# DMA transposes of 16-bit words in place of TensorE transposes for eight of eleven FFN blocks, in a two-layer decoder trunk

## The chip, the cores and the metric

The kernel runs on one core of a Trainium2 chip. Five engines work beside each other, each through its own queue in order: TensorE (PE, matmuls; its weight loads are shown as PEld), VectorE (DVE), ScalarE (ACT), GpSimd (POOL) and SyncE (SP, which only issues DMAs). Sixteen DMA engines move data. The metric is the device time of one execution in microseconds, of which the median of three runs is taken.

## The reference

Two layers over 256 tokens of width 2048, all in float32:

```python
for l in range(DEPTH):                                   # DEPTH = 2
    h = rms_norm(x, norm1_g[l])
    z = h @ w_in[l]                                      # 2048 -> 3584
    z_sgu = jax.nn.gelu(z[..., :2 * SGU_WIDTH], approximate=False)
    out_a = chunked_sgu(z_sgu, sgu_norm_g[l], sgu_w[l], sgu_b[l])
    out_b = swa_sink_attention(..., sinks[l], rel_bias)  # 16 heads, window 128, T5 bias
    mixed = jnp.concatenate([rms_norm(out_a, out_norm_a[l]),
                             rms_norm(out_b, out_norm_b[l])], axis=-1)
    x = x + mixed @ w_out[l]
    h2 = rms_norm(x, norm2_g[l])
    x = x + (jax.nn.silu(h2 @ w_gate[l]) * (h2 @ w_up[l])) @ w_down[l]   # width 5632
return x
```

The relative bias of a head depends on query minus key alone, so a head's 128 x 256 table is one line of values, read at a shift for each query.

## The kernel before

Every product of float32 is made of three matmuls in a reduced format (`mm3`, L143 to L146): both operands are split into a high and a low part, and high x high, high x low and low x high are added up in PSUM. Activations are split when they are made. Weights are split as they come: `raw_load` (L89) brings 512 KB (128 partitions x 1024 columns), `split2` (L96) has ACT write `wh` (a cast, L102) and DVE write `wl` (the difference, L103). There are seven `raw` buffers and five each of `wh` and `wl`. A **unit** is one such load, its split and its matmuls.

The FFN has 11 blocks of 512 hidden columns. Blocks 2 to 10 (`S_BLOCKS`) are made by `seven`, which forms both token halves with seven products of half the size in place of eight: its units (`s_unit`) have six matmuls, on tiles `m0` to `m4`, and some of its weights are sums of loads that DVE adds up (L676, L677, L685) and that a DMA from POOL adds into (L688). Blocks 0 and 1 are made by `half`, on tiles `dacc`, with standard units of 12 matmuls, and so is the down projection, `down`, over groups of one to three blocks.

When a block's gated activations `sg` (two tiles of 128 tokens x 512 columns) are ready, they must be turned, so that the hidden columns lie on the partitions, and split. `act_T` (L613) does that for half a block: four TensorE transposes into the PSUM tile `ps_f`, a cast on ACT (L617) and a subtraction on DVE (L618) that make one pair `aT`. `act_later` (L640) asks for it two and three ticks after the block. A tick is a standard unit; an `s_unit` counts half.

What runs when is decided as the program is written out. The loop at L807 takes pieces of `seven` in turn, and `debt` counts DVE's estimated time (`vec`) up and PE's (`pe`) down; while it is above zero, standard units of `std_stream` are put between, since they have much PE time for one split. A piece of `down` is possible only when both `aT` pairs of all its blocks exist (L791), and otherwise a later piece or none is taken. `held`, `room` and `admit` keep no more than six `aT` pairs alive. What was written out is then ordered on each engine by a scheduler, and each engine runs its list in order.

Once at the start, `rel_table` (L261) makes the bias: three small loads, a matmul that picks table rows (`ps_r`), an addition, a store of one line per head to DRAM (`rline`) and a skewed copy DRAM to DRAM of 2 MB (`rdram`), which `load_bias` reads with 512 KB loads, twice four in all.

At the end `down` adds `acc` to the residual `xres` and stores 256 KB pieces (L768, L771).

Of the kernel before, what the change touches and what calls it, by code (L numbers as in the profile page):

```python
# [12 lines left out]
F32 = mybir.dt.float32  # L13
F32R = mybir.dt.float32r
BF16 = mybir.dt.bfloat16
AF = mybir.ActivationFunctionType
ALU = mybir.AluOpType
AX = mybir.AxisListType
PSUM = bass.MemoryType.PSUM
DRAM = bass.MemoryType.DRAM  # L20
# [15 lines left out]
NB = 512  # L36
KT = D // P
EPS = 1e-6
NEG = -1e30
NI = 3584 // NB  # L40
NFF = DFF // NB
ND = D // NB
# [28 lines left out]
def trunk(ctx, tc, x, xt, w_in, w_out, w_gate, w_up, w_down, sgu_w, sgu_g, consts,  # L71
          rel_bias, onehot, radd, out):
    nc = tc.nc

    cp = ctx.enter_context(tc.tile_pool(name="cp", bufs=1))
# [4 lines left out]
    sp = ctx.enter_context(tc.tile_pool(name="sp", bufs=4))  # L80
    dp = ctx.enter_context(tc.tile_pool(name="dp", bufs=1, space=DRAM))
    pa = ctx.enter_context(tc.tile_pool(name="pa", bufs=5, space=PSUM))
# [3 lines left out]
    def f(t):  # L86
        return t.bitcast(F32)
# [27 lines left out]
    def pe(n):  # L115
        debt[0] -= n * MM * LOAD
# [4 lines left out]
    def later(delay, fn):  # L121
        pending.append((clock[0] + delay, next(serial), fn))
# [122 lines left out]
    xres = cp.tile([P, NTOK, D], F32, tag="xres", name="xres")  # L245
    rdram = dp.tile([NH, P, SEQ], F32, tag="rdram", name="rdram")
    pairs1 = []
# [12 lines left out]

    def rel_table():  # L261
        relb = cp.tile([NBUCKET, NH], F32, tag="relb", name="relb")
        nc.gpsimd.dma_start(relb, rel_bias)
        oneh = zp.tile([NBUCKET, RL], F32, tag="z", name="oneh")
        nc.gpsimd.dma_start(oneh, onehot)
        rad = zp.tile([NH, RL], F32, tag="z", name="rad")
        nc.gpsimd.dma_start(rad, radd)
        ps_r = small_ps([NH, RL], "ps_r")
        nc.tensor.matmul(ps_r, relb, oneh, start=True, stop=True)
        rsb = zp.tile([NH, RL], F32, tag="z", name="rsb")  # L270
        nc.vector.tensor_tensor(rsb, ps_r, rad, ALU.add)
        rline = dp.tile([NH, RL], F32, tag="rline", name="rline")
        nc.sync.dma_start(rline, rsb)
        skew = bass.AP(
            tensor=rline.tensor, offset=rline.offset + P - 1, ap=[[RL, NH], [-1, P], [1, SEQ]]
        )
        nc.sync.dma_start(rdram, skew)

    first_pair(0)
    for p in range(1, KT // 2):  # L280
        later(p, lambda p=p: first_pair(p))
    for i in range(2 * NTOK):
        later(5 + 2 * i, lambda i=i: load_x(i // 2, i % 2))
    later(11, rel_table)

    for lay in range(L):
# [75 lines left out]
        def attend(g, t, kT=kT, qT=qT, vhl=vhl, ov=ov, bias=bias, layer=layer, pts=pts):  # L362
            nkb = t + 1
            nk = nkb * P
            k0 = SEQ - nk
            G = g // 2
# [246 lines left out]
        def act_T(b, c, sg, pairs_f=pairs_f):  # L613
            ps = pm.tile([P, 2, SEQ], F32, tag="sm", name="ps_f")
            transpose_pair([sg[t][:, 2 * c * P : (2 * c + 2) * P] for t in range(NTOK)], ps)
            pair = pair_tile("aT")
            nc.scalar.copy(pair[:, 0], ps)  # L617
# [137 lines left out]
        def down(blocks, n, final, lay=lay, pairs_f=pairs_f, norm_block=norm_block, ss1=ss1,  # L755
# [10 lines left out]
            for t in range(NTOK):  # L766
                xs = xres[:, t, n * NB : (n + 1) * NB]
                nc.vector.tensor_tensor(xs, acc[t], xs, ALU.add)  # L768
                vec(1, VEC_P)
                if final and lay == L - 1:  # L770
                    nc.sync.dma_start(out[t * P : (t + 1) * P, n * NB : (n + 1) * NB], xs)  # L771
            if final and lay < L - 1:
# [135 lines left out]
```

## Time and profile before

| | |
|---|---|
| median of 3 runs | 1932.12 us (1931.79 to 1932.31) |
| the profiled execution | 1932.53 us, span 1930.8 us, granted clock 0.999 |
| busy, share of the span | PE 100%, PEld 81%, DVE 88%, ACT 60%, POOL 6% |
| DMA | 424.39 MB, 220 GB/s over the span |
| transposes of `ps_f` | 176 of 8734 matmuls |
| FFN of layer 0, of layer 1 | about 290 to 965 us, 1250 to 1926 us |

The page names an instruction by line, engine, operation and tiles (out<-in). A group shows its count, the time it was busy, the mean of one in ns and the engine's idle time just before it with what ended most of it. PE's matmuls overlap, so that one shows 0.39 us where the next starts 0.23 us later.

### The profile page before, as it was taken

The page shows a single profiled execution, that of the slowest core. Times are in us where ns is not written, and L with a number is a line of the kernel's source. Part 1 is how long each engine was busy: PE and PEld are TensorE (multiplying, and loading weights), DVE is VectorE, ACT ScalarE, POOL GpSimd, SP SyncE. Part 2 cuts the span into 40 slices and gives each one's busy share as a digit, 9 for nine tenths or more (in the row PEclk, how much of TensorE's full clock was granted, in tenths as well). Part 3 has the DMA queues.
Part 4 walks back from the last instruction along what each step waited for, and adds up shares of the span by engine and source line. Part 5 has one row for each costly group of instructions (what it writes and reads, how often), then busy time and mean ns, then how long its engine had stood idle before and what let it go on. Part 6 is the DMA issues. An engine that isn't in the chain of part 4 may idle for free.

```text
span 1930.8 us, 24275 instructions
## 1 busy us (share of the span) xinstructions
PE 1922.1 (100%) x8734; PEld 1568.0 (81%) x8734; DVE 1698.7 (88%) x1896; ACT 1162.8 (60%) x1475; POOL 122.8 (6%) x127
## 2 busy tenths in 40 slices
PE   9999999999999999999999999999999999999999
PEld 7777888888888888888888788888888888888887
DVE  6787689999999999999767866899999999999995
ACT  7476566666665665656555765666665565665662
POOL 1211000000000000000012100000000000000000
PEclk9999999999999999999999999999999999999999
DMA  8845557768768777767555445577678678768773
GB/s 324 287 156 174 175 172 253 218 218 262 220 217 260 227 225 246 227 224 248 206 205 190 162 165 186 184 240 224 214 238 241 217 240 251 231 219 246 238 240 121
DMA packets 119704, 424.39 MB, mean 220 GB/s; under 512 B 13168, under 2 KB 15344, under 8 KB 119584
## 3 DMA queue, kind: packets, MB, share of 16 engines
q1 hardware_dynamic: 106928, 377.57, 54.6%
q0 software_dynamic: 12512, 45.19, 12.7%
q8 instruction: 68, 1.11, 0.2%
q14 instruction: 52, 0.43, 0.1%
q10 hardware_dynamic: 144, 0.08, 0.0%
HBM read 420.66 MB, written 4.23 MB: 220 GB/s over the span
## 4 chain that ended last, share of the span: by engine, by line
PE 94%; DVE 3%; ACT 1%; issue 1%; DMA 1%; POOL 0%; SPq 0%; ACTq 0%; DVEq 0%; POOLq 0%
PE m L145 11%; PE m L146 11%; PE m L144 11%; PE dacc L144 10%; PE dacc L145 10%; PE dacc L146 10%; PE acc L144 9%; PE acc L146 9%; PE acc L145 9%; DVE wl L103 1%; PE ps_f L217 1%; PE ps_n L217 1%; PE ps_s L379 0%; PE ps_p L414 0%; PE ov L422 0%
## 5 line engine op out<-in xcount | busy, mean ns | idle before, releaser
L102 ACT CAST wh<-raw 128x1024 fp32r<-128x1024 f32 (+1 forms) x778 | 799.8, 1049 | 592.1 <-DVE raw L676 198.6
L103 DVE TENSOR_TENSOR wl<-raw,wh 128x1024 fp32r<-128x1024 f32 (+1 forms) x778 | 926.2, 1219 | 130.3 <-ACT wh L102 124.3
L145 PE MATMUL dacc<-wl,aT 128*128 128x512 f32 x576 | 225.4, 391 | 0.0
L144 PE MATMUL dacc<-wh,aT 128*128 128x512 f32 x576 | 224.8, 391 | 0.0
L145 PE MATMUL m<-wl,ext 128*128 128x512 f32 x576 | 224.8, 390 | 0.0
L146 PE MATMUL dacc<-wh,aT 128*128 128x512 f32 x576 | 224.6, 390 | 0.0
L144 PE MATMUL m<-wh,ext 128*128 128x512 f32 x576 | 224.5, 392 | 0.0
L146 PE MATMUL m<-wh,ext 128*128 128x512 f32 x576 | 224.3, 389 | 0.0
L103 DVE TENSOR_TENSOR wl<-t,wh 128x1024 fp32r<-128x1024 f32 x144 | 175.6, 1222 | 25.1 <-ACT wh L102 21.5
L102 ACT CAST wh<-t 128x1024 fp32r<-128x1024 f32 x144 | 151.2, 1052 | 57.8 <-PE dacc L146 37.9
L144 PE MATMUL acc<-wh,hT 128*128 128x512 f32 x448 | 179.5, 402 | 0.4 <-ACT pt L415 0.4
L145 PE MATMUL acc<-wl,hT 128*128 128x512 f32 x448 | 175.2, 391 | 1.1 <-DVE wl L103 1.1
L146 PE MATMUL acc<-wh,hT 128*128 128x512 f32 x448 | 175.2, 391 | 0.0
L144 PE MATMUL m<-wh,hT 128*128 128x512 f32 x432 | 168.5, 390 | 0.1
L145 PE MATMUL m<-wl,hT 128*128 128x512 f32 x432 | 168.1, 389 | 0.0
L146 PE MATMUL m<-wh,hT 128*128 128x512 f32 x432 | 168.1, 389 | 0.0
L144 PE MATMUL acc<-wh,aT 128*128 128x512 f32 x384 | 152.0, 396 | 0.0
L146 PE MATMUL acc<-wh,aT 128*128 128x512 f32 x384 | 150.0, 391 | 0.0
L145 PE MATMUL acc<-wl,aT 128*128 128x512 f32 x384 | 149.7, 390 | 0.0
L688 POOL DMA_DIRECT2D t<-in_w_gate_dram x72 | 61.3, 852 | 1326.1 <-DVE wl L103 828.3
L145 PEld LDWEIGHTS dacc<-wl,aT 128*128 128x128 f32 x576 | 108.2, 188 | 24.1 <-DVE wl L103 2.2
L144 PEld LDWEIGHTS dacc<-wh,aT 128*128 128x128 f32 x576 | 108.1, 188 | 23.8 <-DVE xres L768 1.4
(150 smaller groups left out, 2809.0 us busy)
## 6 DMA issues: line engine op xcount, KB each, us to landing
raw<-in_w_gate_dram SPq DMA_DIRECT2D x176, 512.0 KB, 5.5
raw<-in_w_up_dram SPq DMA_DIRECT2D x176, 512.0 KB, 4.5
raw<-in_w_down_dram SPq DMA_DIRECT2D x176, 512.0 KB, 4.8
raw<-in_w_in_dram SPq DMA_DIRECT2D x108, 512.0 KB, 4.3
t<-in_w_gate_dram POOLq DMA_DIRECT2D x72, 512.0 KB, 6.3
raw<-in_w_out_dram SPq DMA_DIRECT2D x64, 512.0 KB, 3.2
bias<-rdram POOLq DMA_DIRECT2D x8, 512.0 KB, 4.4
raw<-in_w_in_dram SPq DMA_DIRECT2D x8, 256.0 KB, 5.4
```

The costliest lines, as they stand in the source:

```text
L102: nc.scalar.copy(wh[:, j : j + step, :], src)
L103: nc.vector.tensor_tensor(wl[:, j : j + step, :], src, f(wh[:, j : j + step, :]), ALU.subtract)
L144: nc.tensor.matmul(acc, ah, wh, start=first, stop=False, **more)
L145: nc.tensor.matmul(acc, ah, wl, start=False, stop=False, **more)
L146: nc.tensor.matmul(acc, al, wh, start=False, stop=last, **more)
L217: nc.tensor.transpose(ps[:, j, t * P : (t + 1) * P], blocks[t][:, j * P : (j + 1) * P], ident)
L688: nc.gpsimd.dma_start(t2, w_gate[lay, b, i, 1], accum_op=ALU.add)
```

## The change

`BY_PE = (5, 9, 10)`: these three blocks are turned as before. For the other eight, `act_later` first has ACT copy each `sg` tile, seen as 16-bit words, into `cut`, with all low words ahead of all high words (128 x 1024 words), and a DMA issued from ACT's queue transposes it, eight squares of 128 x 128 words, into `turned`. Five and six ticks later, in place of two and three, `act_T` has ACT put the words back together with four copies of 128 x 256 words for each half block, into the float32 tile `xT` in SBUF. The cast and the subtraction then read `xT` and no longer PSUM. `pe(2)` is counted for the three blocks alone.

`rel_table` is gone: the host lays out the line of each head (`rel_line`), reversed, so that `load_bias` reads it with a shift of one element a partition, and the addition in `attend` walks the columns backwards. `turns` starts at 1, which leaves the rotation of the small PSUM tiles after it as it was. Of the very last output tile, the two column halves are added and stored apart, the second store from ACT's queue.

```diff
+BY_PE = (5, 9, 10)
...
-    turns = itertools.count()
+    turns = itertools.count(1)
...
-    later(11, rel_table)
...
         def load_bias(g, bias=bias):
             bt = ap.tile([P, GRP, SEQ], F32, tag="big", name="bias", bufs=8)
-            nc.gpsimd.dma_start(bt, rdram[g * GRP : (g + 1) * GRP].rearrange("h q k -> q h k"))
+            skew = bass.AP(
+                tensor=rel_line.tensor, offset=rel_line.offset + g * GRP * RL + RL - P - SEQ + 1,
+                ap=[[1, P], [RL, GRP], [1, SEQ]],
+            )
+            nc.gpsimd.dma_start(bt, skew)
...
-                    s[:, r::2, :], halves[r], 1.0 / math.sqrt(HD), bias[g][:, r::2, k0:],
+                    s[:, r::2, :], halves[r], 1.0 / math.sqrt(HD), bias[g][:, r::2, :nk][:, :, ::-1],
...
         def act_T(b, c, sg, pairs_f=pairs_f):
-            ps = pm.tile([P, 2, SEQ], F32, tag="sm", name="ps_f")
-            transpose_pair([sg[t][:, 2 * c * P : (2 * c + 2) * P] for t in range(NTOK)], ps)
+            if b in BY_PE:
+                xT = pm.tile([P, 2, SEQ], F32, tag="sm", name="ps_f")
+                transpose_pair([sg[t][:, 2 * c * P : (2 * c + 2) * P] for t in range(NTOK)], xT)
+                pe(2)
+            else:
+                xT = zp.tile([P, 2, SEQ], F32, tag="z", name="xT")
+                dst = xT.bitcast(U16).rearrange("p j (q w) -> p w j q", w=2)
+                for t in range(NTOK):
+                    src = sg[t].rearrange("p (w j) q -> p w j q", w=2)
+                    for w in range(2):
+                        nc.scalar.copy(
+                            dst[:, w, :, t * P : (t + 1) * P], src[:, w, 2 * c : 2 * c + 2, :]
+                        )
             pair = pair_tile("aT")
-            nc.scalar.copy(pair[:, 0], ps)
-            nc.vector.tensor_tensor(pair[:, 1], ps, f(pair[:, 0]), ALU.subtract)
+            nc.scalar.copy(pair[:, 0], xT)
+            nc.vector.tensor_tensor(pair[:, 1], xT, f(pair[:, 0]), ALU.subtract)
             vec(1, VEC_P)
-            pe(2)
...
         def act_later(b, sg, held=held, admit=admit):
+            sg = list(sg)
+            if b not in BY_PE:
+                for t in range(NTOK):
+                    cut = zp.tile([P, 2, NB], U16, tag="z", name="cut")
+                    nc.scalar.copy(cut, sg[t].bitcast(U16).rearrange("p (n w) -> p w n", w=2))
+                    sg[t] = zp.tile([P, 2 * NB // P, P], U16, tag="z", name="turned")
+                    nc.scalar.dma_start_transpose(sg[t], cut.rearrange("p w n -> p (w n)"))
...
-                later(2 + c, lambda c=c: come(c))
+                later((2 if b in BY_PE else 5) + c, lambda c=c: come(c))
...
-                    nc.sync.dma_start(out[t * P : (t + 1) * P, n * NB : (n + 1) * NB], xs)
+                    if end:
+                        queue = nc.sync if c == 0 else nc.scalar
+                        queue.dma_start(out[t * P : (t + 1) * P, n * NB + c : n * NB + c + w], xs)
```

On PE, in the FFN of the first layer, a seven-product unit (`m_3207`) was followed by half a block's four transposes and then by a standard unit on `dacc`, before:

```order
L146 MATMUL m_3207<-wh,ext 128x512
L217 MATMUL ps_f<-ident,m_3039 128x128
L217 MATMUL ps_f<-ident,u_3041 128x128
L217 MATMUL ps_f<-ident,m_3039 128x128
L217 MATMUL ps_f<-ident,u_3041 128x128
L144 MATMUL dacc_3052<-wh,hT 128x512
L145 MATMUL dacc_3052<-wl,hT 128x512
```

PE's list of the change has no such rows there: units follow each other, 128 rows on `ps_f` are gone and 48 (of 176) stay.

On ACT, at the end of block 6 in the first layer, stood before, from the first SiLU (`m`, then `u`) to the second `aT` cast:

```order
L717 ACTIVATE m_5355<-m_4931,ir_2594 128x512
L102 CAST wh<-raw 128x1024 x4
L717 ACTIVATE u_5357<-u_5357,ir_2600 128x512
L102 CAST wh<-t_5521 128x1024
L102 CAST wh<-raw 128x1024
L617 CAST aT<-ps_f 128x512
L102 CAST wh<-raw 128x1024
L617 CAST aT<-ps_f 128x512
```

After the change the same block's stretch begins so, with `cut` and the transposes between the casts:

```order
L718 ACTIVATE m_5447<-m_5005,ir_2578 128x512
L102 CAST wh<-raw 128x1024
L638 COPY cut<-m_5447 128x1024
L102 CAST wh<-raw 128x1024
L640 DMA_TRANSPOSE turned<-cut 128x8x128
L718 ACTIVATE u_5449<-u_5449,ir_2584 128x512
L102 CAST wh<-raw 128x1024
L102 CAST wh<-t_5603 128x1024
L638 COPY cut<-u_5449 128x1024
L102 CAST wh<-raw 128x1024
L640 DMA_TRANSPOSE turned<-cut 128x8x128
```

and goes on, the next rows, with the joins (the first two of the four read the first transpose's tile, the other two the second's):

```order
L102 CAST wh<-raw 128x1024 x2
L607 COPY xT<-turned 128x2x128 x4
L102 CAST wh<-raw 128x1024
L611 CAST aT<-xT 128x512
L607 COPY xT<-turned 128x2x128 x4
L102 CAST wh<-raw 128x1024
L611 CAST aT<-xT 128x512
```

Nine `wh` casts, two copies into `cut`, two issues and eight joins stand there now. In eight of the sixteen turned blocks only two casts lie between the second transpose and the joins, in two blocks four, in six ten or more.

On DVE, at the end of block 7's first part in the first layer, before (with buffer numbers; the splits `wl_5911` and `wl_6046` belong to units on `dacc`, the eight between them to seven-product units, the last two of which lie beyond these rows):

```order
L103 TENSOR_TENSOR wl_5911<-raw_5908,wh_5910 128x1024
L103 TENSOR_TENSOR wl_5927<-raw_5853,wh_5926 128x1024
L103 TENSOR_TENSOR wl_5937<-raw_5851,wh_5936 128x1024
L698 TENSOR_TENSOR u1_5948<-m3_5625,m1_5946 128x512
L103 TENSOR_TENSOR wl_5960<-raw_5957,wh_5959 128x1024
L701 TENSOR_TENSOR c12_5950<-m1_5539,u1_5948 128x512
L748 SCALAR_TENSOR_TENSOR sg_3945<-dacc0_5574,ir1_2594,sg_3945 128x512
L748 SCALAR_TENSOR_TENSOR sg_3947<-dacc1_5575,ir1_2600,sg_3947 128x512
L103 TENSOR_TENSOR wl_5972<-raw_5969,wh_5971 128x1024
L103 TENSOR_TENSOR wl_5982<-t2_5521,wh_5981 128x1024
L702 TENSOR_TENSOR c22_5951<-m2_5648,c12_5950 128x512
L103 TENSOR_TENSOR wl_5994<-raw_5991,wh_5993 128x1024
```

After the change, the last 12 rows of the same block's run without a unit on `dacc`:

```order
L103 TENSOR_TENSOR wl_5950<-t2_5925,wh_5949 128x1024
L103 TENSOR_TENSOR wl_5961<-raw_5923,wh_5960 128x1024
L103 TENSOR_TENSOR wl_5971<-raw_5921,wh_5970 128x1024
L699 TENSOR_TENSOR u1_5982<-m3_5669,m1_5980 128x512
L103 TENSOR_TENSOR wl_5992<-raw_5989,wh_5991 128x1024
L702 TENSOR_TENSOR c12_5984<-m1_5621,u1_5982 128x512
L103 TENSOR_TENSOR wl_6004<-raw_6001,wh_6003 128x1024
L703 TENSOR_TENSOR c22_5985<-m2_5692,c12_5984 128x512
L103 TENSOR_TENSOR wl_6014<-t2_5603,wh_6013 128x1024
L704 TENSOR_TENSOR c12_5984<-m4_5681,c12_5984 128x512
L103 TENSOR_TENSOR wl_6034<-raw_6031,wh_6033 128x1024
L612 TENSOR_TENSOR aT_6028<-xT_6023,aT_6028 128x512
```

The run now begins earlier and has 13 splits (these seven, five ahead of them and `wl_6044` behind) before the next unit on `dacc`, which reads the pair `aT_6028` of the last row. Ahead of these rows stand four adds of 1024 columns and the two products `sg` of the standard block, and behind `wl_6044` the second `aT`.

More of the change, by code (lines that the diff above doesn't have):

```diff
@@ L259, in load_x @@
             sum_sq(ss[t][:, n : n + 1], xres[:, t, n * NB : (n + 1) * NB])
[L261 to L277, printed above, removed]
     first_pair(0)
@@ L766, in down @@
             for t in range(NTOK):
-                xs = xres[:, t, n * NB : (n + 1) * NB]
-                nc.vector.tensor_tensor(xs, acc[t], xs, ALU.add)
+                end = final and lay == L - 1
+                w = NB // 2 if end and n == ND - 1 and t == NTOK - 1 else NB
+                for c in range(0, NB, w):
+                    xs = xres[:, t, n * NB + c : n * NB + c + w]
+                    nc.vector.tensor_tensor(xs, acc[t][:, c : c + w], xs, ALU.add)
+                    if end:
+                        queue = nc.sync if c == 0 else nc.scalar
+                        queue.dma_start(out[t * P : (t + 1) * P, n * NB + c : n * NB + c + w], xs)
                 vec(1, VEC_P)
-                if final and lay == L - 1:
-                    nc.sync.dma_start(out[t * P : (t + 1) * P, n * NB : (n + 1) * NB], xs)
             if final and lay < L - 1:
@@ L874 @@
     )
-    m = np.arange(RL)
-    dist = 2 * P - 1 - m
+    dist = 2 * P - RL + np.arange(RL)
     valid = (dist >= 0) & (dist < WIN)
-    onehot = ((np.arange(NBUCKET)[:, None] == _bucket(dist)[None]) & valid[None]).astype(np.float32)
-    radd = np.broadcast_to(np.where(valid, 0.0, NEG).astype(np.float32), (NH, RL))
+    line = np.where(valid, a["rel_bias"][_bucket(dist)].T, np.float32(NEG))
     down = a["w_down"].reshape(L, NFF, 2, 2, P, ND, NB).transpose(0, 1, 5, 2, 4, 3, 6)
```

11 lines of the change are left out of this document (3 added, 8 removed).

## The prediction

> **What bounds the kernel now.** I read the page's busy times first, then busy time by stretches, then who waited for whom.
>
> ```profile
> span 1930.8 us, 24275 instructions
> PE 1922.1 (100%) x8734; PEld 1568.0 (81%) x8734; DVE 1698.7 (88%) x1896; ACT 1162.8 (60%) x1475; POOL 122.8 (6%) x127
> PE 94%; DVE 3%; ACT 1%; issue 1%; DMA 1%; POOL 0%; SPq 0%; ACTq 0%; DVEq 0%; POOLq 0%
> ```
>
> TensorE (PE) is busy in all but 8.7 us of the span, and 94% of the chain that ended last is its work. So time taken off PE counts in full wherever nothing else is nearly as late. What is nearly as late shows by stretches (columns: length, then busy us of PE, PEld, DVE, ACT and POOL with instruction counts, clock, DMA share, GB/s):
>
> ```profile
> 60.00:120.00 60.00, 58.93 (x299) 45.53 (x298) 49.73 (x80) 35.36 (x70) 12.91 (x10) 1.00 0.66 229
> 600.00:700.00 100.00, 100.00 (x448) 82.29 (x447) 96.68 (x95) 62.26 (x67) 4.26 (x5) 1.00 0.74 241
> 800.00:900.00 100.00, 100.00 (x447) 82.74 (x446) 97.65 (x95) 61.33 (x64) 5.11 (x6) 1.00 0.79 249
> 900.00:965.00 65.00, 64.93 (x296) 53.36 (x295) 47.98 (x53) 36.46 (x49) 0.00 (x0) 1.00 0.59 209
> ```
>
> In the FFN, VectorE (DVE) is busy 97 of 100 us beside a full PE; only in the last 65 us of a layer's FFN, when the seven-product blocks are done, does it fall to 74%. ScalarE (ACT) stands at 62%. The FFN therefore has two limits 3% apart, and what joins them is the supply of split weights:
>
> ```profile
> L102 ACT CAST wh<-raw 128x1024 fp32r<-128x1024 f32 (+1 forms) x778 | 799.8, 1049 | 592.1 <-DVE raw L676 198.6
> ACT wh L102 <- PE acc L146: 149.2, 100, 3.1
> ACT wh L102 <- PE dacc L146: 147.4, 95, 5.6
> PE acc L145 <- DVE wl L103: 1.1, 2, 0.6
> ```
>
> ACT idles 592 us before its casts, some 300 of it because PE has not yet freed one of the five `wh` buffers, while PE waited for a `wl` for 1.1 us in all. The split weights run ahead of PE nearly always, by at most four units.
>
> **What goes: 128 transposes on PE.** One group of four, and the next, with the matmuls round them (start, duration):
>
> ```profile
> 350.82 0.39 PE L146 MATMUL m<-wh,hT 128*128 128x512 f32 x1
> ...
> 352.18 0.39 PE L146 MATMUL m<-wh,ext 128*128 128x512 f32 x1
> ...
> 352.41 0.27 PE L217 MATMUL ps_f<-ident,m 128*128 128x128 f32 x1
> ...
> 352.74 0.27 PE L217 MATMUL ps_f<-ident,u 128*128 128x128 f32 x1
> ...
> 353.08 0.39 PE L145 MATMUL dacc<-wl,hT 128*128 128x512 f32 x1
> ...
> 355.36 0.40 PE L146 MATMUL dacc<-wh,hT 128*128 128x512 f32 x1
> ...
> 356.27 0.40 PE L145 MATMUL m<-wl,ext 128*128 128x512 f32 x1
> ```
>
> Six matmuls lie between 350.82 and 352.18: a step of 0.227 us, so 1.36 us for a unit of a seven-product block and 2.72 for a unit of 12. Two steps would take 0.45 us; from 352.18 to 353.08 they take 0.90 and from 355.36 to 356.27 0.91. A group of four costs 0.45 to 0.46 us (not 4 x 0.27: they overlap). Eight blocks, two groups each, two layers are 32 groups: **-14.7 us**. The removed work stands between matmuls on a full engine, so nothing hides it.
>
> **The bias table: -1.2 us.** PE ran it in the middle of its work:
>
> ```profile
> 37.33 0.39 PE L146 MATMUL acc<-wh,hT 128*128 128x512 f32 x1
> 37.65 1.03 PE L269 MATMUL ps_r<-oneh,relb 32*16 32x512 f32 x2
> ...
> 38.94 0.40 PE L145 MATMUL acc<-wl,hT 128*128 128x512 f32 x1
> ```
>
> 1.61 us where two steps are 0.45: 1.16 us. SP loses two issues and the DMA engines a 2 MB copy. PE's 1.07 us of idle in the stretch from 60 to 120 might go with that copy or not: 0 to 1.1 more, of which I take nothing. The bias loads keep their size and row length.
>
> **The last output: -0.3 us.**
>
> ```profile
> 1925.89 0.39 PE L146 MATMUL acc<-wh,aT 128*128 128x512 f32 x1
> 1926.36 1.01 SPq L771 DMA_DIRECT2D out_dram<-xres  x2
> ```
>
> From the last matmul's end at 1926.28 to the span's end are 4.5 us, of which the add of 0.68 us and the landing of 256 KB are the chain. The halves cost DVE some 0.1 us more and land half the bytes last: between 0.6 less and 0.3 more.
>
> **Where the standard units come late: +4.5 us.** The pairs are now asked for five ticks after the block instead of two, so `down` units become possible later. The DVE rows in the change section show one such place: between two units on `dacc`, PE has 13 units of a seven-product block in a row, where before had eight. DVE pays this much an instruction:
>
> ```profile
> 392.60 3.49 DVE L103 TENSOR_TENSOR wl<-raw,wh 128x1024 fp32r<-128x1024 f32 x3
> 1909.51 1.28 DVE L768 TENSOR_TENSOR xres<-acc,xres 128x512 f32<-128x512 f32 x2
> ```
>
> That is (3.49 - 1.22) / 2 = 1.14 us for 1024 columns and 0.60 for 512. The run holds 13 splits, 4 adds of 1024 and 8 instructions of 512: 17 x 1.14 + 8 x 0.60 = 24.2 us against PE's 13 x 1.36 = 17.7. DVE falls 6.5 us behind (the eight of before, with six instructions of 512: 12.7 against 10.9); the lead it can have is four units, 5.4 us. A second run in each layer, of 14 units, falls behind by about 5.3. So PE idles between 6.5 - 5.4 = 1.1 us a layer (full lead at both) and 11.8 (no lead). I take 2.25, nearer the full lead, because PE waited so little for `wl` so far: +4.5 for two layers, range 2 to 24.
>
> **ACT's new work: +4.8 us.** None of the new instructions is in the trace; the nearest rows:
>
> ```profile
> L307 ACT COPY vhl<-zkv 128x256 f32<-128x256 f32 x4 | 1.6, 404 | 0.0
> L527 ACT CAST hT<-g 128x512 fp32r<-128x512 f32 x16 | 10.0, 622 | 0.5
> L617 ACT CAST aT<-ps_f 128x512 fp32r<-128x512 f32 x44 | 25.6, 582 | 15.3 <-PE ps_f L217 15.1
> L717 ACT ACTIVATE m<-m,ir 128x512 f32<-128x512 f32 x18 | 12.4, 691 | 13.7 <-PE m L146 13.7
> 384.66 2.95 ACT L102 CAST wh<-raw 128x1024 fp32r<-128x1024 f32 x3 [2.80 <-DVE raw L676]
> 0.81 0.41 ACTq L170 DMA_DIRECT2D cst<-in_consts_dram  x1
> ...
> L688 POOL DMA_DIRECT2D t<-in_w_gate_dram x72 | 61.3, 852 | 1326.1 <-DVE wl L103 828.3 <-DVE tot L228 175.8 <-ACT wh L102 163.0
> ```
>
> A cast of 1024 columns steps by (2.95 - 1.05) / 2 = 0.95 us. A block's two `cut` copies are as wide: 1.9. Eight joins of 256 columns at 0.40: 3.2. Casts from SBUF for casts from PSUM: 2 x 0.04. Two issues, bounded by ACT's own 0.41 and POOL's 0.85: 0.8. Together 6.0 us a block, 96 us in all: ACT goes to 65% on average. But it falls in one place. Over the ACT rows of after in the change section, from the first SiLU to the second `aT` cast, ACT has nine casts (8.6), SiLUs (1.4) and this work: 17.1 us, where the same list before made 11.2. PE needs 6 x 1.36 + 3 x 2.72 = 16.3 us for these nine units. The slack of 5 us is gone, and ACT waits there besides, in order: for PE's bank before the first SiLU (13.7 / 18 = 0.8 us), for DVE's products before a `cut`, for a landing before the joins. Behind the waiting instruction stand the next `wh`, DVE's `wl` behind that, then PE. The lead covers most: 0 to 1.5 us a block. I take 0.3, 16 x 0.3 = 4.8, near nothing because ACT idles so much. DVE's own `aT` subtract from SBUF costs what it cost from PSUM: nothing.
>
> **The sum.** -14.7 - 1.2 - 0.3 + 4.5 + 4.8 = -6.9 us. The profiled execution took 1932.53 us, 1.7 outside its span, and the runs' median is 1932.12, 0.4 below it; I take the sum off the median: **1925.2 us**. A difference of 0.2% (3.9 us) is about what a measurement of this kernel tells from none.
>
> **Rivals.** *Nothing is given back beyond a full lead:* 1932.1 - 14.7 - 1.2 - 0.3 + 2.2 = 1918. DVE's 97% speaks against it. Chance 0.06.
>
> *ACT is held at each issue.* If a transpose holds ACT as POOL's DMA holds POOL, 0.85 us, or longer, a block's ACT work passes PE's by 1.7 us or more, and DVE cannot win it back before the next block, since 3% of 60 us is 1.8. Half of 0.9 us more for 16 blocks is 7 us: 1932, within 0.2%. In the trace ACT issued one DMA, in 0.41. Chance 0.26. [...]
>
> *The turned words land late: slower.* In half of the blocks only two casts and two joins (2.7 us) lie between the second issue and the first join of its tile. Landings from issue:
>
> ```profile
> xr<-in_xt_dram SPq DMA_DIRECT2D x8, 256.0 KB, 6.0
> rdram<-rline SPq DMA_DIRECT2D x1, 2048.0 KB, 14.7
> out_dram<-xres SPq DMA_DIRECT2D x8, 256.0 KB, 2.5
> ```
>
> A transpose moves 256 KB, the size of the loads at 6.0 and the stores at 2.5. The skewed copy, 2048 rows of 1 KB in 14.7 us, is the nearest for small rows: 1024 rows at that pace are 7.4 us, and two follow each other. Up to 2.7 plus a lead of 3 to 4 us nothing happens; past some 6.5 us ACT stands at the join and PE runs dry. At 9 us, 2.5 us a block in 8 blocks is 20 us more: 1946. Chance 0.22. [...]
>
> **How the numbers follow.** The forecast has 0.46, with a range of its own from 1918 to 1928; with the rival at 1918, faster by over 0.2% (under 1928.3) has 0.52. Within 0.2% is ACT held: 0.26. Slower is late landing: 0.22. The range goes from 1916 to 1946: the low end takes the best of the gaps, tail and start, the high end the late landings at 9 us.
>
> **What would show it.** No `ps_f` on PE but in blocks 5, 9 and 10, and six matmul steps still 1.36 us. PE idle of 2 to 3 us a layer in the 13-unit run, put down to DVE `wl`. ACT's issue rows near 0.4 us, the landings under 6 us, and ACT's wait before the first join small. I am wrong if PE's idle in the FFN stays under 2 us (then 1918), if an issue row is over 1 us, or if ACT waits for `turned` by microseconds in many blocks.

## The result, and the profile after

| | before | after |
|---|---|---|
| median beside each other, 4 runs each | 1932.21 us (1931.79 to 1932.50) | 1955.39 us (1951.96 to 1958.05) |
| the profiled execution | 1932.53 us | 1951.96 us |
| PE's rows on `ps_f` | 176 | 48 |

The change made the kernel slower by 23 us, a ratio of 1.0121 [1.0109, 1.0133]. The forecast was 1925.2 us, 7 us faster, with a range from 1916 to 1946.

The page of after: span, busy times, and the shares of the chain that ended last.

```profile
span 1949.9 us, 24205 instructions
...
PE 1922.2 (99%) x8604; PEld 1555.7 (80%) x8604; DVE 1698.9 (87%) x1896; ACT 1236.5 (63%) x1635; POOL 122.0 (6%) x124
...
PE 74%; DVE 12%; ACT 5%; issue 4%; DMA 3%; ACTq 1%; POOL 0%; DVEq 0%; SPq 0%; POOLq 0%
```

PE does 130 matmuls less, and the chain of the end, 94% PE before, has lost 20 points to DVE, ACT, issues and DMAs. PE's busy time hardly shows this: a wait counts there only in part (the matmul at 680.71 us below comes 2.65 us later than a normal step would bring it, and 2.49 us of that are shown as idle). The stretches of after, with the columns as in the prediction, show it:

```profile
60.00:120.00 60.00, 59.84 (x304) 46.62 (x303) 49.06 (x82) 34.76 (x77) 11.91 (x9) 1.00 0.51 169
600.00:700.00 100.00, 95.45 (x405) 75.89 (x404) 93.32 (x91) 68.23 (x83) 5.00 (x6) 0.98 0.83 239
800.00:900.00 100.00, 98.24 (x430) 79.45 (x429) 94.11 (x91) 59.78 (x69) 5.11 (x6) 1.00 0.76 240
900.00:965.00 65.00, 65.00 (x292) 53.66 (x291) 56.37 (x58) 39.24 (x44) 1.70 (x2) 1.00 0.72 236
```

From 600 to 700 PE got through 405 matmuls instead of 448, and DVE, 97% busy before, did 91 instructions instead of 95. DVE's missing work turns up from 900 to 965, where it was 47.98 us and is 56.37. At 97% it had 3 us in 100 left to make up what it once stood idle.

Who waited for whom in after (us in total, times, the longest):

```profile
DVE wl L103 <- ACT wh L102: 166.0, 168, 3.6
...
PEld m L145 <- DVE wl L103: 15.7, 25, 1.4
...
PEld dacc L144 <- ACT wh L102: 10.4, 13, 1.7
...
PEld m L144 <- ACT wh L102: 7.9, 10, 2.9
...
ACT xT L607 <- DMA turned<-cut: 7.1, 8, 1.8
```

The new instructions (count, shortest, median and longest ns; then the time from issue to landing):

```profile
L607 ACT COPY xT<-turned x128: 466/473/492, 352.5 to 1774.7; 128x256 uint16<-128x256 uint16 x128
L640 ACTq DMA_TRANSPOSE turned<-cut x32: 1247/1250/2371, 343.9 to 1767.0; - x32
...
DMA to landing us min/median/max: 3.1/4.7/10.6
```

One issue takes ACT's queue 1.25 us, where the prediction counted 0.41, and a join takes 0.473, where it had 0.404. The four landings over 6 us (7.1 to 10.6) are those of block 1 in the two layers; the other 28 stay under 6.

The largest stall in the first layer, in the time line of after. It stands where two `cut` copies and two issues of a standard block follow each other on ACT:

```profile
673.43 1.05 ACT L638 COPY cut<-sg 128x1024 uint16<-128x1024 uint16 x1 [0.85 <-DVE sg L749]
674.51 1.52 ACTq L640 DMA_TRANSPOSE turned<-cut  x1
676.07 1.05 ACT L638 COPY cut<-sg 128x1024 uint16<-128x1024 uint16 x1 [1.59 <-DVE wl L103]
677.15 2.37 ACTq L640 DMA_TRANSPOSE turned<-cut  x1
679.62 1.04 ACT L102 CAST wh<-raw 128x1024 fp32r<-128x1024 f32 x1 [2.50 <-DVE t L678]
...
680.71 0.50 PE L144 MATMUL m<-wh,ext 128*128 128x512 f32 x1 [2.49 <-ACT wh L102]
681.97 0.79 PE L145 MATMUL m<-wl,ext 128*128 128x512 f32 x1 [0.76 <-DVE wl L103]
```

This is block 1. For 6.2 us, from 673.4 to 679.6, ACT makes no `wh`. The 2.50 us ahead of the cast aren't idle time: the second issue fills them, though the row names DVE. PE has used up its lead and stops for 2.49 us, then for 0.76. Then comes a second loss, in the stretches of after:

```profile
681.80:685.20 3.40, 3.23 (x8) 2.55 (x9) 3.40 (x4) 3.35 (x5) 0.72 (x1) 0.50 1.09 173
```

For 3.4 us the granted clock is 0.50. There are three such periods in after before its last matmul, each behind a stall, and none in before.

To compare kernels I add up PE's steps (from one matmul's start to the next one's) over each whole trace. A step of the three-matmul product is 0.227 us; a step of over 0.40 us counts as **waiting**, with all of its time above 0.227.

| first matmul to last | before | after |
|---|---|---|
| steps on `ps_f` | 16.3 us | 5.7 |
| the bias matmul `ps_r` | 1.0 | 0 |
| waiting | 3.7 (7 steps) | 29.0 (44) |
| what half clock adds | 0 | 4.7 |
| small excess of the other product steps | 21.3 | 22.1 |

Sum of the differences: -10.6 - 1.0 + 25.3 + 4.7 + 0.8 = +19.2; the last matmul ended 18.9 us later, at 1945.19 instead of 1926.28, and the rest of the two lists differs by the 0.3 us between. From the last matmul to the span's end it is 4.7 us instead of 4.5. The profiled execution of after is the fastest of its four.

### The profile page after: what moved, and what is told of

It reads as the page before. It is cut to its first block, busy times and chain, and to the rows that moved or that the text cites. A ratio compares the mean times of both kernels' runs of the same rounds, so it can differ in the third digit from the quotient of the medians.

```text
span 1949.9 us, 24205 instructions
## 1 busy us (share of the span) xinstructions
PE 1922.2 (99%) x8604; PEld 1555.7 (80%) x8604; DVE 1698.9 (87%) x1896; ACT 1236.5 (63%) x1635; POOL 122.0 (6%) x124
## 4 chain that ended last, share of the span: by engine, by line
PE 74%; DVE 12%; ACT 5%; issue 4%; DMA 3%; ACTq 1%; POOL 0%; DVEq 0%; SPq 0%; POOLq 0%
PE acc L144 8%; PE acc L145 8%; PE acc L146 8%; PE dacc L144 8%; PE dacc L145 8%; PE dacc L146 8%; PE m L145 8%; PE m L146 8%; PE m L144 8%; DVE wl L103 6%; ACT wh L102 3%; DMA turned<-cut 2%; DVE raw L677 1%; ACT cut L638 1%; DVE t L678 1%
## 5 line engine op out<-in xcount | busy, mean ns | idle before, releaser
L145 PE MATMUL dacc<-wl,aT 128*128 128x512 f32 x640 | 249.9, 390 | 2.2 <-DVE wl L103 2.1
L144 PE MATMUL dacc<-wh,aT 128*128 128x512 f32 x640 | 249.4, 392 | 2.0 <-ACT wh L102 1.9
L146 PE MATMUL dacc<-wh,aT 128*128 128x512 f32 x640 | 249.3, 390 | 0.0
L103 DVE TENSOR_TENSOR wl<-t,wh 128x1024 fp32r<-128x1024 f32 x144 | 175.5, 1221 | 17.9 <-ACT wh L102 15.3
L144 PEld LDWEIGHTS dacc<-wh,aT 128*128 128x128 f32 x640 | 119.7, 188 | 30.8 <-ACT wh L102 4.2
L145 PEld LDWEIGHTS dacc<-wl,aT 128*128 128x128 f32 x640 | 120.1, 188 | 29.7 <-DVE wl L103 5.1
L146 PEld LDWEIGHTS dacc<-wh,aT 128*128 128x128 f32 x640 | 120.1, 188 | 24.9
L145 PEld LDWEIGHTS m<-wl,ext 128*128 128x128 f32 x576 | 108.7, 189 | 36.2 <-DVE wl L103 13.9
L144 PEld LDWEIGHTS m<-wh,ext 128*128 128x128 f32 x576 | 109.4, 190 | 30.7 <-ACT wh L102 7.9
```

Source lines behind the costliest of these rows:

```text
L103: nc.vector.tensor_tensor(wl[:, j : j + step, :], src, f(wh[:, j : j + step, :]), ALU.subtract)
L144: nc.tensor.matmul(acc, ah, wh, start=first, stop=False, **more)
L145: nc.tensor.matmul(acc, ah, wl, start=False, stop=False, **more)
L146: nc.tensor.matmul(acc, al, wh, start=False, stop=last, **more)
```

## The experiments

Each kernel was timed beside the kernel before on the same chip, whose medians there were 1932.4 to 1932.9. All edits are against the changed kernel, unless another is named. Five kernels leave out the turning or don't use its result (`e3_nodma`, `e5_nowork`, `e6_early`, `e7_hold`, `e9_plan`): they show what a part costs and are no kernels to use.

**What the parts apart from the transposes do (`e1_parts`).** All eleven blocks turned by PE.

```diff
-BY_PE = (5, 9, 10)
+BY_PE = tuple(range(NFF))
```

> All eleven blocks turned by TensorE, with the host-laid bias line and the halved last output kept: the change without its DMA transposes. Theory (the loss is made at the turned blocks alone): TensorE loses the bias matmul's 1.0 to 1.2 us and the tail moves by 0.2 at most, so 1930.5 to 1931.5 us. Rival (the bias line or the split last store has a hidden cost, for instance the reversed read of the bias on VectorE): 1934 us or more.

1930.76 us (1930.46 to 1931.53), ratio 0.999 [0.9981, 0.9999]: the bias line and the halved output save 1.9 us. In its trace the last matmul ends 2.1 us earlier than before, and from there to the span's end it is 4.5 us, as before: the bias line is the gain, the halves give nothing. In this trace PE is busy for 60.00 us of the stretch from 60 to 120, where it was 58.93: the idle time there, of which the prediction took nothing, went with the table. This kernel is the base for what follows.

**Only the late asks (`e2_late`).** The same, but the pairs of the eight blocks are asked for after 5 and 6 ticks; PE still turns them.

```diff
-                later((2 if b in BY_PE else 5) + c, lambda c=c: come(c))
+                later((2 if b in (5, 9, 10) else 5) + c, lambda c=c: come(c))
```

> As e1_parts, with TensorE turning all blocks, but the eight blocks of the change are asked for five and six ticks after the block and not two and three. Only the plan is that of late pairs; no DMA transpose, no copies. Theory A (ScalarE's new work and its held issues make the loss): 0 to 3 us over e1_parts, from the run of 14 seven-product units that the plan has once a layer. Theory B (late pairs starve the standard stream and make most of the loss): 12 us or more over e1_parts, about 1943 us.

1936.33 us, ratio 1.002 [1.0011, 1.003]: 5.6 us over the base, between the two theories. Waiting went from 2.4 to 5.2 us, and the steps on `ps_f` from 16.3 to 19.5, two of which stand 1.0 us each for a `wh`. These two and the four longest new waits in the FFN, 3.9 us together, lie in block 1's run of 14 seven-product units (from 695 and from 1658 us).

**Without the DMA (`e3_nodma`).** The joins read `cut` itself, so that nothing is issued or awaited; the words aren't turned.

```diff
-                    sg[t] = zp.tile([P, 2 * NB // P, P], U16, tag="z", name="turned")
-                    nc.scalar.dma_start_transpose(sg[t], cut.rearrange("p w n -> p (w n)"))
+                    sg[t] = cut.rearrange("p w (j q) -> p (w j) q", q=P)
```

> The change with the DMA transposes left out: the joins read the copied words untransposed, so the hidden activations of eight blocks are not turned. ScalarE keeps its 32 copies and 128 joins, the delays stay, the 32 issues of 1.25 us on ScalarE's queue and the landings go. Theory A1 (the held issues make the loss): 1925 to 1933 us, 20 us or more below the change. Theory A2 (the copies and joins, 6.4 us a block on ScalarE, make it): 1945 us or more. Theory B (late pairs): 1945 us or more, with TensorE waiting in the runs of 13 and 14 units.

1931.88 us, ratio 0.9997 [0.9987, 1.0006]: 23.5 us under after. The copies stay; issue and landing are the loss, as theory A1 had it. Nor do the transposes hold back the weights: a `raw` load lands 4.6 us after its issue in after and 4.7 here, at the median, and ACT waits for `raw` 13.7 us in after and 14.7 here.

**The issues on SP (`e4_sp`).**

```diff
-                    nc.scalar.dma_start_transpose(sg[t], cut.rearrange("p w n -> p (w n)"))
+                    nc.sync.dma_start_transpose(sg[t], cut.rearrange("p w n -> p (w n)"))
```

> The change with the 32 transposes issued from SyncE's queue and not from ScalarE's; all else stays, landings included. Theory A1 (ScalarE held 1.25 us at each issue): 1928 to 1938 us, TensorE's waits for wh near gone. Rival (a transpose that waits on SyncE for ScalarE's copy holds the weight loads behind it): 1950 us or more, with ScalarE waiting for raw. Theory A2 or B: as the change, 1950 to 1956.

1940.13 us (1938.89 to 1941.84), ratio 1.0039 [1.0024, 1.0054]: 15.3 under after, and still slower than before. That is 2 us more than theory A1 allowed and far from the others. An issue takes as long there (1.23 us), but nothing of the weights' split stands behind it.

**Neither DMA nor copies (`e5_nowork`).** No `cut`, no issue, no joins; the cast reads `sg` unturned, at the late ticks.

> The change's plan with nothing put in the place of the transposes: no copy into cut, no DMA transpose, no joins; the cast and the subtraction read one untransposed activation tile, so the hidden activations of eight blocks are not turned. The late asks at five and six ticks stay. From e3_nodma (1931.9) this takes ScalarE's copies and joins. Theory A2 (the copies and joins have their price where ScalarE, VectorE and TensorE are level): 1920 to 1925 us, 7 to 12 below e3_nodma. Theory B2 (what e3_nodma still lost is the late plan): 1929 us or more.

1929.04 us, ratio 0.9982 [0.9973, 0.9991]: `cut` and joins cost only 2.8 us. That is theory B2's time, but not for its reason, as the next kernel shows: the late plan isn't what is left to gain.

**The transposes simply gone (`e6_early`).** The same, asked for at 2 and 3 ticks as before the change.

```diff
-                later((2 if b in BY_PE else 5) + c, lambda c=c: come(c))
+                later(2 + c, lambda c=c: come(c))
```

> As e5_nowork, but asked at two and three ticks as before the change: the transposes taken away and nothing added or moved. This is the most the change could save. By the step counts on TensorE (16.3 to 5.7 us on ps_f, some 3 us more in the steps behind the groups) 1916 to 1919 us, against 1930.8 for e1_parts. If the late plan costs the 5.6 us of e2_late here too, e5_nowork stands 4 to 7 above this run; if late pairs cost nothing without transposes, the two are within 2.

1929.26 us (1928.07 to 1930.86), ratio 0.9983 [0.9974, 0.9992]: a miss, and the one that counts most. 128 transposes are gone, nothing takes their place, and the kernel is only 1.5 us under the base. The trace has PE waiting for 15.1 us, where the base had 2.4. One such place, in the time line of this kernel:

```profile
668.00 0.68 DVE L605 TENSOR_TENSOR aT<-sg,aT 128x512 fp32r<-128x512 f32 x1
...
668.61 1.22 DVE L667 TENSOR_TENSOR raw<-raw 128x1024 f32<-128x1024 f32 x1
...
669.74 0.68 DVE L605 TENSOR_TENSOR aT<-sg,aT 128x512 fp32r<-128x512 f32 x1
...
669.93 1.05 ACT L102 CAST wh<-raw 128x1024 fp32r<-128x1024 f32 x1 [3.46 <-DVE raw L667]
670.34 1.22 DVE L668 TENSOR_TENSOR t<-raw 128x1024 f32<-128x1024 f32 x1
...
671.03 0.49 PE L144 MATMUL m<-wh,ext 128*128 128x512 f32 x1 [0.73 <-ACT wh L102]
...
671.48 1.22 DVE L103 TENSOR_TENSOR wl<-raw,wh 128x1024 fp32r<-128x1024 f32 x1
...
672.75 0.50 PE L144 MATMUL m<-wh,ext 128*128 128x512 f32 x1 [1.22 <-ACT wh L102]
```

ACT is named, but ACT waited 3.46 us for DVE, and DVE isn't idle for a moment: it makes four other things between two `wl`. With the products `pe(2)` of the eight blocks no longer counted, the account that sets the order thinks PE has less to do and puts the standard units, in which DVE can catch up, in other places. In layer 0 the program now has a run of 14 seven-product units with 5.3 us more DVE than PE work, by the prediction's prices, and two of 10 with 3.7 and 3.1; the base has none over 10 with 1.9. But long runs are only a part of it: the place shown lies in a run of seven units behind block 1, where two products `sg`, two `aT` and three adds fall together, and the run of 14 (from 843 us) has 0.4 us of waiting inside and 1.9 some 14 us behind it.

**Joins that don't wait for the landing (`e7_hold`).** The transposes are issued on ACT, but the joins read `cut`, so the words used aren't turned.

```diff
-                    sg[t] = zp.tile([P, 2 * NB // P, P], U16, tag="z", name="turned")
-                    nc.scalar.dma_start_transpose(sg[t], cut.rearrange("p w n -> p (w n)"))
+                    turned = zp.tile([P, 2 * NB // P, P], U16, tag="z", name="turned")
+                    nc.scalar.dma_start_transpose(turned, cut.rearrange("p w n -> p (w n)"))
+                    sg[t] = cut.rearrange("p w (j q) -> p (w j) q", q=P)
```

> The change with its 32 transposes issued from ScalarE as before, but the joins read the copied words and not the turned ones, so nothing waits for a landing; the hidden activations of eight blocks are not turned. Theory A1 (holding ScalarE at the issue is the loss): 1948 us or more, near the change. Rival (the wait for the landing is the loss): 1932 to 1938 us, near e3_nodma.

1944.86 us, ratio 1.0065 [1.0048, 1.0081]: 13.0 over the kernel without the DMA, 10.5 under after, between the two theories. Both the hold at the issue and the dependence on the landing cost, about alike. (In the trace of after the joins' own waits for `turned` are 7.1 us. No row of this kernel waits for a transpose, so full buffers don't show as a cause here.)

**The copies on GpSimd, the issues on SP (`e8_pool`).**

```diff
-                        nc.scalar.copy(
+                        nc.gpsimd.tensor_copy(
...
-                    nc.scalar.copy(cut, sg[t].bitcast(U16).rearrange("p (n w) -> p w n", w=2))
+                    nc.gpsimd.tensor_copy(cut, sg[t].bitcast(U16).rearrange("p (n w) -> p w n", w=2))
```

> The change with all its ScalarE work moved: the 32 copies and 128 joins on GpSimd (busy 6%), the transposes issued from SyncE. Theory A (ScalarE's work and holds are the loss): 1922 to 1934 us if GpSimd's copies run near the 1.19 us of its 128x1024 select and don't stand behind its DMA waits. Rival (GpSimd's queue, whose DMAs wait up to 41 us for VectorE, delays the turned pairs, or its copies slow VectorE): 1940 us or more, with TensorE waiting for aT or VectorE's wl above 1222 ns.

1976.54 us, ratio 1.023 [1.0215, 1.0245], the slowest of all. The rival's time, and its sign: a `cut` copy takes 1.9 us there instead of 1.04, and something else shows in DVE's splits, in the view of tile `wl` of this kernel:

```profile
L103 DVE TENSOR_TENSOR wl<-raw,wh x778: 684/1218/4289, 4.8 to 1956.5; 128x1024 fp32r<-128x1024 f32 x194, 128x512 fp32r<-128x512 f32 x1
```

The longest `wl` takes 4.29 us (1.23 before). 22 splits take over 1.5 us, and each of the 22 overlaps a GpSimd copy. DVE's same 1896 instructions are busy 1739.7 us instead of 1698.9: GpSimd's help is paid for by the engine that has nothing to spare. The rival's other half shows as well: ACT waits 33.0 us for GpSimd's joins. What each of the two costs wasn't separated.

**The same order as before, the transposes gone (`e9_plan`).** The sixth kernel with one line: the two products are counted for every pair.

```diff
             vec(1, VEC_P)
+            pe(0 if b in BY_PE else 2)
```

> e6_early (the 128 transposes left out, the gated activations of eight blocks enter the second product unturned, with their first delay of 2 and 3 ticks), and the planner still counts two products for each aT, as before. So the standard units keep the places they have in e1_parts, where the longest run of seven-product units without a unit of dacc or acc is 10 with 1.9 us more VectorE work than TensorE work in it; in e6_early there was one of 14 with 5.3 and two of 10 with 3.7 and 3.1. Theory P, e6_early stayed at 1929 only since the account without those products pulled units of dacc ahead and left long runs in which VectorE falls behind: the waits of 15.1 us fall to about 3 to 5 and the time is 1917 to 1921. Theory D, VectorE is a limit of its own some 1% behind TensorE, so what leaves TensorE comes back as waits whatever the order: 1926 to 1931, waits of 10 or more.

1919.22 us (1918.60 to 1919.55), ratio 0.993 [0.9914, 0.9947]: theory P. Two of its stretches:

```profile
600.00:700.00 100.00, 99.59 (x438) 81.75 (x437) 97.15 (x96) 62.38 (x67) 3.97 (x5) 1.00 0.74 230
800.00:900.00 100.00, 100.00 (x446) 82.73 (x445) 95.96 (x93) 59.48 (x62) 5.12 (x6) 1.00 0.79 251
```

Waiting is 5.7 us. So the transposes were worth 11.5 us and DVE could nearly follow; 10.0 of it hung on one line of the planner's account.

**That line in the changed kernel (`e10_afterplan`).**

> The changed kernel with one line more: two products are counted for each aT of the eight blocks too. The longest runs of seven-product units stay 14 (5.6 us of VectorE more than TensorE) and 10 (1.9, 1.3), in place of 14 (5.3), 13 (5.7) and 10 (3.7). Theory P, the order of the standard units costs about as much as the late turning: 8 to 12 us under the changed kernel, 1943 to 1947. Theory H, the seven microseconds in which ScalarE cuts, issues two transposes and makes no wh are the cost: within 3 us of the changed kernel, 1952 to 1958.

1964.01 us (1961.75 to 1966.64), ratio 1.0163 [1.0147, 1.0178]: 8.6 slower, against both theories. What saved 10 us alone costs here. Its largest stall, on ACT and PE in the time line of this kernel:

```profile
696.30 0.69 ACT L719 ACTIVATE m<-m,ir 128x512 f32<-128x512 f32 x1 [0.16 <-PE m L146]
699.08 1.05 ACT L639 COPY cut<-m 128x1024 uint16<-128x1024 uint16 x1 [2.08 <-DMA turned<-cut]
702.60 1.25 ACTq L641 DMA_TRANSPOSE turned<-cut  x1
703.89 0.72 ACT L719 ACTIVATE u<-u,ir 128x512 f32<-128x512 f32 x1 [3.77 <-issue]
704.52 1.03 ACT L102 CAST wh<-raw 128x1024 fp32r<-128x1024 f32 x1
...
705.60 0.80 PE L144 MATMUL m<-wh,ext 128*128 128x512 f32 x1 [5.26 <-ACT wh L102]
```

`cut` waits 2.08 us for an earlier block's transpose, whose tiles come from the same pool `zp` of eight buffers, and the issue begins 2.5 us after `cut` is done; no releaser is named for that, and by the code it too needs a buffer of the pool. From 696.3 to 704.5, for 8.2 us, no `wh` is made, and PE stops for 5.3 us (4.1 at the same place in layer 1). The earlier block is block 1: in `STD_ORDER` its standard unit is followed at once by the `down` unit that needs its pairs, so its late turning holds up the standard units behind it.

**That line, and the issues on SP (`e11_sp_plan`).**

> e10_afterplan with the transposes issued on SP instead of ScalarE. If what e4_sp saved (15 us) and what the counted products save are two costs, they add: with theory P 1928 to 1933, with theory H 1938 to 1941. If both only removed the same stalls, 1936 to 1941 with either. Faster than the kernel before only if under 1930.

1937.51 us (1935.33 to 1941.34), ratio 1.0027 [1.0016, 1.0037]: 26.5 under the last kernel, but only 2.6 under the kernel with the issues on SP alone. The two edits removed the same stalls for the most part, as the last of the three forecasts had it.

**Block 1 by PE again (`e12_block1_sp` and `e13_block1`).** The last two kernels, with the run of 14 gone from the order (longest: 10, 1.9 us).

```diff
-BY_PE = (5, 9, 10)
+BY_PE = (1, 5, 9, 10)
```

Issues on SP:

> e11_sp_plan with block 1 turned by TensorE again (seven blocks by DMA). Block 1's activations are wanted in the unit that follows its own standard unit, so its late turning is what makes the run of 14 seven-product units; with it on TensorE the longest run is 10 with 1.9 us, as before the change. If the order of the standard units and ScalarE's queue are the two costs (theory P+H): the waits fall from 20.8 to 8 to 12, TensorE pays 1.5 more for sixteen transposes, and the time is 1925 to 1930, under the kernel before. If the turned blocks cost their stalls wherever they stand (theory S, each by its own copies and landings): 1934 to 1938.

Issues on ACT:

> The same with the transposes issued on ScalarE as in the changed kernel (e10_afterplan with block 1 turned by TensorE). e10_afterplan stood still for 5.3 us at 700 and 4.3 at 1676, in block 1's run. Theory P+H: 1932 to 1942, about half of the loss against e12_block1_sp's kernel being the issues on ScalarE. Theory S: 1952 or more.

1934.27 (1931.96 to 1936.23), ratio 1.001 [1.0001, 1.0019], and 1946.93 (1944.25 to 1948.36), ratio 1.0073 [1.006, 1.0085]. With the issues on ACT block 1 was worth 17.1 us, and the stall of 5.3 us is gone; the result lies between the theories. On SP it was worth 3.2: theory P+H missed by 4 us, and the time is the one that theory S gave. There, counted by steps as above, 9.7 of 16.4 us of waiting lay within 7 us behind a join. DVE at one of them, in the time line of the kernel on SP:

```profile
351.72 3.48 DVE L103 TENSOR_TENSOR wl<-raw,wh 128x1024 fp32r<-128x1024 f32 x3
356.49 0.69 DVE L612 TENSOR_TENSOR aT<-xT,aT 128x512 fp32r<-128x512 f32 x1 [1.28 <-ACT aT L611]
357.10 1.22 DVE L103 TENSOR_TENSOR wl<-raw,wh 128x1024 fp32r<-128x1024 f32 x1
358.54 0.69 DVE L612 TENSOR_TENSOR aT<-xT,aT 128x512 fp32r<-128x512 f32 x1 [0.23 <-ACT aT L611]
```

DVE stands idle for 1.28 us at the first `aT`, since ACT reached the joins before the words had landed; PE stops at 361.6 and at 362.8, for 0.59 and 0.77 us.

**The asks later and apart (`e14_asks_later`).** The kernel with block 1 by PE and the issues on SP; the asks after 7 and 9 ticks.

```diff
-                later((2 if b in BY_PE else 5) + c, lambda c=c: come(c))
+                later((2 + c) if b in BY_PE else (7 + 2 * c), lambda c=c: come(c))
```

> e12_block1_sp, whose asks for the two aT of a turned block come 7 and 9 ticks after it is stored instead of 5 and 6; the order of the standard units and their runs stay the same (10 with 1.9 us). In e12_block1_sp 9.3 of 24 us of waits follow the joins: ScalarE waited for the landing (3.9 us, 4 times), then made both aT in one piece of about 4 us, and VectorE, which takes each wh in turn, lost that time too. Theory L, landing and pile-up: the waits after joins go down to 3 or less and the time is 1925 to 1930. Theory W, the joins' work itself (2.5 us of ScalarE for each aT) stalls wherever it stands: 1932 to 1936.

**1926.02 us (1925.44 to 1927.63), ratio 0.9966 [0.9952, 0.9979]**: theory L, and faster than the kernel before and the changed one. DVE at the same block, in the time line of this kernel:

```profile
352.15 4.83 DVE L103 TENSOR_TENSOR wl<-raw,wh 128x1024 fp32r<-128x1024 f32 x4
356.95 0.69 DVE L612 TENSOR_TENSOR aT<-xT,aT 128x512 fp32r<-128x512 f32 x1
357.56 1.22 DVE L678 TENSOR_TENSOR raw<-raw 128x1024 f32<-128x1024 f32 x1
358.70 0.69 DVE L612 TENSOR_TENSOR aT<-xT,aT 128x512 fp32r<-128x512 f32 x1
```

DVE no longer stops there, and PE waits within 7 us behind a join for 3.4 us in place of 9.7. So theory S, that each turned block costs its stalls wherever it stands, falls: it was when the asks stood. ACT still waits for landings, 5.0 us in all (3.9 with the asks after 5 and 6), in a kernel 8.3 us faster: the length of that wait alone doesn't set the time.

**The cuts a tick apart (`e15_cuts_apart`).** The same, with the second token half cut and issued one tick after the first.

> e14_asks_later, and the second token tile of a block is cut and issued one tick after the first. Theory L: what is left at the cuts (2.2 us in e12_block1_sp) is small, so 0 to 2 us under e14_asks_later, 1924 to 1930. Rival: the later second landing meets the first ask again and gives the time back, 1930 to 1934.

1926.52 us (1924.86 to 1927.74), ratio 0.9966 [0.9954, 0.9979]: no difference, and not the rival.

**The best order, the issues back on ACT (`e16_issue_act`).**

> e14_asks_later with its 28 transposes issued on ScalarE instead of SP, nothing else. Theory I, an issue holds ScalarE for 1.25 us and what is queued behind it comes late: between e12_block1_sp and e13_block1 this was 12.7 us, so 1934 to 1940. Theory Q, in e13_block1 it cost so much only since the asks stood right behind the issues: now under 4 us, 1926 to 1930.

1938.97 us (1930.72 to 1943.81, a wide spread), ratio 1.0025 [1.0013, 1.0037]: theory I, 13.0 us over the issues on SP at the median, 4.7 with the shortest of the twelve.

## Why the prediction was wrong

The base, five of these kernels and after form a chain, each with one thing more:

| step | medians | us |
|---|---|---|
| bias line and halves | before to 1930.8 | -1.9 |
| 128 transposes away, order held | to 1919.2 | -11.5 |
| the two products no longer counted | to 1929.3 | +10.0 |
| asks after 5 and 6 ticks | to 1929.0 | -0.2 |
| `cut` and joins on ACT | to 1931.9 | +2.8 |
| the transposes issued from ACT | to 1944.9 | +13.0 |
| joins wait for the landing | to 1955.4 | +10.5 |

The sum is +22.7, against 23.2 measured (1955.39 - 1932.21). The sizes belong to this sequence: the steps don't add freely, as the line that saves 10 us without the DMA and costs 8.6 with it shows.

**-14.7 for the transposes.** For PE the price was right: from the base to the kernel with the order held, the steps on `ps_f` fall by 11.9 us and the small excess of the product steps by 2.7, 14.6 together. But waiting rises by 3.3, so 11.5 were left, and "nothing hides it" was nearly right only there. The prediction saw that DVE stands 3% behind PE, but didn't ask what the missing `pe(2)` does to the account that decides the order. That gave 10.0 of the 11.5 back.

**-1.2 and -0.3.** Shown together as -1.9, all of it on the bias side: 1.0 us for the step of `ps_r`, and the idle time from 60 to 120 us.

**+4.5 for late standard units.** Alone, on the base, 5.6 us: the size was right. In the chain the same asks cost nothing, since the order had been spoilt already; in after they set up the run at block 1. In the two runs of 13 units that the prediction named, PE waits 4.9 and 4.1 us; half of the 9.0 stands before a `wl`, as forecast, and half before a `wh` that ACT makes late.

**+4.8 for ACT's new work: the step that failed.** The copies were nearly right (2.8 measured). The issue was taken at 0.41 us from ACT's one small DMA; it is 1.25. "The lead covers most" fell with it: at block 1 two issues and two `cut` copies in a row keep `wh` away from DVE and PE for 6 us, more than the lead of four units (5.4 us). Of the 29.0 us of waiting, 6.6 stand right behind these two places; the rest are stalls of 1.5 us or less, nearly all in the FFN, where a DVE that is 97% busy didn't win them back. The issues alone cost 12.7 to 26.5 us in five pairs of kernels: 15.3 in after, 26.5 with the products counted, 12.7 with block 1 by PE, 13.0 with the best order, and 13.0 from the kernel without a DMA to the one whose joins don't wait (there with the transfers themselves). The terms for issue and landing came to 23.5 us (1955.39 - 1931.88) where 4.8 stood for everything.

**The rivals.** "ACT is held at each issue" was the right mechanism: an issue row over 1 us was named as proof, and it came. Its price, half of 0.9 us for 16 blocks, was half of what it cost: 7 against 13. "The turned words land late" happened as well: a landing takes 4.7 us in the middle and 10.6 at most, and waiting for it makes 10.5 us of the loss. The long ones, block 1's, fall where the DMA engines are busy 99% (670 to 680 us) and 97% (1640 to 1650). Each was given a time as if the other didn't happen; together, and with the order, they ended 9 us above the range. For the landing the prediction had 2.5 us (the stores) and 6.0 (the loads), both of 256 KB, and 7.4 at the pace of the skewed copy's rows; the trace has 3.1 at best, counted from the start of an issue of 1.25 us, and 4.7 in the middle. With 3.1 to 10.6 us for the same 256 KB, it depends on more than its size.

Two things stay open. Why the products, counted in the changed kernel, cost 8.6 us is shown only so far that the largest stalls lie in block 1's run and go away with it (in its trace waiting is 39.8 us instead of 29.0, and half clock adds 6.2 instead of 4.7); that the pool of eight buffers makes the stall was read from the trace and not tried with more buffers. What brings the clock to a half is not settled either.

## What to carry to other kernels

An engine saved was time saved only where the next engine was given the same order of work (11.5 us here with it, 1.5 without): before counting a removed instruction as a gain, look at what else reads its cost. A DMA's issue took time of the engine that issued it, and not the same for each kind (on ACT 1.25 us for a transpose, 0.41 for the one plain load); keep it off an engine whose queue holds what the full engines wait for. And where two engines are both nearly full (100% and 97% here), look for single idle gaps on the second one, not at its sum: behind a gap of 1.28 us there the first stopped for 0.59 and 0.77 us (`e12_block1_sp`).

## What the runs showed of the hardware

- A transpose of 128 x 1024 16-bit words takes its issuing queue 1.25 us on ACT and 1.23 to 1.24 on SP, at the median; from issue to landing it takes 3.1 to 10.6 us in after, 4.7 at the median; where SP issues it, 3.8 (`e4_sp`), 3.7 (`e14_asks_later`) and 3.1 (`e8_pool`) at the median; once 16.4 in `e16_issue_act`.
- After some stalls of PE the granted clock is 0.50 for 3.4 us: three times in after (4.7 us of the loss), never before the last matmul in the three fastest kernels. Behind the stall of 5.3 us in `e10_afterplan` it was 10.2 us, behind the one of 4.1 us 6.8. The length of the stall alone doesn't decide: idle gaps of 0.66 and 1.21 us in a row had such a period behind them in `e5_nowork`, gaps of 0.73 and 1.22 us at the same place in `e6_early` had none.
- Beside GpSimd copies, single VectorE splits took up to 4.29 us instead of 1.23.
- The joins, which write every second 16-bit word, took 0.473 us, where a copy of as many float32 columns took 0.404.
